# A batched matrix product in fp32: weights of four matrices in one load, quarter-lane casts on two engines, and no block around the engine programs

## The chip, the cores and the metric

The kernel runs on one core of a Trainium2 chip. A core has engines that run their own instruction streams and meet through semaphores: TensorE (matrix products, PE in the profile, with its weight loads as PEld), VectorE (DVE), ScalarE (ACT), GpSimd (POOL) and SyncE (SP), and 16 DMA engines that move data between HBM and the on-chip memory SBUF. Matrix products land in a second on-chip memory, PSUM. The metric is the device time of one execution in microseconds, as the median over runs.

## The reference

```python
def setup_inputs():
    b1, b2, m, k, n = 8, 16, 256, 512, 384
    return {
        "x": np.random.randn(b1, b2, m, k).astype(np.float32),
        "weight": np.random.randn(b1, b2, k, n).astype(np.float32),
    }

def reference(x: np.ndarray, weight: np.ndarray) -> np.ndarray:
    return np.matmul(x, weight).astype(np.float32)
```

There are 128 independent products, each of 256 x 512 by 512 x 384. In bytes: 67 MB of x, 101 MB of weights, 50 MB of output.

## The kernel before

**Tiling.** The 128 matrices are taken in 32 groups (`NG`) of four (`G`). Of one group, x is 1024 rows of 512; each of the 128 partitions holds 8 consecutive rows (`R`), so that 32 partitions (`C`) hold one matrix. A group is worked in four quarters (`T`), each of two rows per partition. The loads are `x_sb` (2 MB, two buffers), and `w_sb` (1.5 MB, four buffers): one load of weights has two matrices (`D`), and in it a partition holds 8 consecutive weight rows, a run of 12 KB. A group has two such loads. The output of a group is one store of 1.5 MB, from four buffers `out_sb`.

**Stages.** For a group n, in the order of the data:

- `cast_x` on ScalarE (lines 125 to 136) turns x from fp32 to bf16 and reorders its columns on the way, in two instructions of 2048 elements per partition. There is one buffer `x_bf`; the wait of line 128 is for the transposes of group n-1.
- `prepare` on VectorE (lines 138 to 157) first casts the weights into `w_bf` (two groups' worth of buffers): eight instructions, each on 64 partitions with 1536 elements. The two halves of a matrix go to the upper and the lower partitions, which makes the order of the contraction index agree with that of x. It waits for the product of group n-2 (line 140) and for each load (line 143).
- `multiply` on TensorE (lines 159 to 187) transposes the four quarters of x, two bf16 values at a time as one fp32 word, into PSUM buffers `pt` (four).
- The second half of `prepare` (lines 152 to 156) copies these transposes to `x_t` in SBUF, a quarter at a time. It stands behind the weight casts on VectorE.
- `multiply` then makes the product: per quarter 32 matmuls, each with a 128 x 32 block of `x_t` as stationary and 128 x 384 of weights as moving operand. The four matrices of a group sit in four column blocks of the array. Results are in two PSUM buffers `po`, so that quarter q+2 waits for the copy-out of quarter q (line 176).
- `copy_out` on ScalarE (lines 190 to 198) moves a quarter to `out_sb`. Behind the second quarter of group n, ScalarE does `cast_x` of group n+1.

**The order of transfers** is written by hand on SyncE, the only issuer (lines 209 to 224). `load` (lines 96 to 113) issues x of a group, then its two halves of the weights; x waits for the cast of x two groups back (line 99), each half of the weights for the casts of that half two groups back (line 107). SyncE issues the loads of groups 0 to 3 (`LAG`), and then for each n the load of group n+4 and the store of group n. The last store goes out in four pieces. All transfers stand in one queue, in the order of issue.

**Frame.** The engine programs are functions inside an `nc.Block()` (line 200), which stands in a critical section of the tile framework (line 54). In the profile, instructions of the section's entry and exit have line 54, those of the block's exit the helper file's line, and those of the program's end line 288.

Of the kernel before, what the change touches and what calls it, by code (L numbers as in the profile page):

```python
# [11 lines left out]
def kernel(  # L12
# [25 lines left out]

# [4 lines left out]
    D = 2  # L43
    S = 2
    HP = P // D
    NG = B // G

    XS, WS, OS = 2, 2 * G // D, 4
    BS, TS, WBS = 1, 2, 2 * G
# [4 lines left out]
    ctx.enter_context(tc.tile_critical())  # L54
# [11 lines left out]
    def sems(name, n):  # L66
# [5 lines left out]

    x_bf = sbuf("x_bf", [P, R, S, HP, KO], bf16, BS)
    x_t = sbuf("x_t", [P, R, KO // 2, P, 2], bf16, TS)
    w_sb = sbuf("w_sb", [P, S * KO, N], fp32, WS)
    w_bf = sbuf("w_bf", [P, KO, N], bf16, WBS)
# [7 lines left out]
    id_done, x_cast, w_cast, t_made, t_copied, p_made, o_copied = (  # L84
        sems(name, 1)[0]
        for name in (
            "id_done", "x_cast", "w_cast", "t_made", "t_copied", "p_made", "o_copied"
# [8 lines left out]
    def load(e, t, U, s):  # L96
        n = t * U + s
        if not isinstance(n, int) or n >= XS:
            e.wait_ge(x_cast, n + (1 - XS))
# [4 lines left out]
        for d in range(G // D):  # L104
            slot = (s * (G // D) + d) % WS
            if not isinstance(n, int) or n >= 2:
                e.wait_ge(w_cast, n * (G * S) + ((d + 1) * D * S - 2 * G * S))  # L107
            e.dma_start(  # L108
                w_sb[slot][:],
                w_rows[bass.ds(n * (G * K) + d * (D * K), D * K)].rearrange(  # L110
                    "(p k) n -> p k n", k=S * KO
                ),
            ).then_inc(w_in[slot], 16)
# [11 lines left out]
    def cast_x(e, t, U, s):  # L125
        n = t * U + s
        e.wait_ge(x_in[s % XS], (t * (U // XS) + s // XS) * 16 + 16)
        e.wait_ge(t_made, n * T + ((1 - BS) * T + BIAS))
        for h in range(S):
            ins = e.copy(  # L130
                out=x_bf[s % BS][:, :, h],
                in_=x_sb[s % XS][:].rearrange("p r (q s c) -> p r s q c", s=S, c=KO)[
                    :, :, h
                ],
            )
        ins.then_inc(x_cast, 1)

    def prepare(e, t, U, s):
        n = t * U + s
        e.wait_ge(p_made, n * T + (BIAS - T))  # L140
        for d in range(G // D):
            slot = (s * (G // D) + d) % WS
            e.wait_ge(  # L143
# [46 lines left out]
    def copy_out(e, t, U, s, q):  # L190
        n = t * U + s
        if q == 0:
# [4 lines left out]
            in_=po[(s * T + q) % PO][:, :, :N],  # L197
        ).then_inc(o_copied, 1)

    block = ctx.enter_context(nc.Block())  # L200

    @block.gpsimd
    def _(e):
# [89 lines left out]
```

## Time and profile before

| | us |
|---|---|
| median of 14 runs (lowest to highest) | 519.99 (519.63 to 520.25) |
| the profiled execution | 520.48 |
| its span, first to last instruction | 518.7 |
| TensorE busy (matmul) | 313.1 |
| VectorE busy | 323.9 |
| ScalarE busy | 212.7 |
| GpSimd busy | 0.7 |

The profile is of one execution. Its span leaves out what lies before the first and after the last instruction, here 1.8 us. A row of the instruction groups reads: line, engine, operation, output<-input, shapes, count | busy us, mean ns of one | idle time of the engine just before, and what ended most of it. The slices cut the span into 40 equal parts of 13 us; each digit is a busy share in tenths.

The transfers by issue, with KB each and the median us from issue to landing, are:

```profile
w_sb<-in_weight_dram SPq DMA_DIRECT2D x64, 1536.0 KB, 27.5
x_sb<-in_x_dram SPq DMA_DIRECT2D x32, 2048.0 KB, 25.9
out_dram<-out_sb SPq DMA_DIRECT2D x31, 1536.0 KB, 30.6
out_dram<-out_sb SPq DMA_DIRECT2D x4, 384.0 KB, 3.9
```

A landing time of some 27 us for transfers that take 4 to 5 us of the engines' time says that a transfer waits in the queue behind others.

### The profile page before, as it was taken

Reading aid. Unit: us, or ns where it says so; the run is one execution under the profiler, and the core shown is the slowest. Engines: PE = TensorE matmul, PEld = TensorE weight load, DVE = VectorE, ACT = ScalarE, POOL = GpSimd, SP = SyncE. Lnnn points to the kernel's source line nnn. Section 1 sums busy time; section 2 is a strip of 40 time slices with the busy share of each in tenths; the row PEclk is TensorE's granted clock in tenths of the full one; section 3 lists DMA queues with packets and bytes.
Section 4 is the critical chain, followed back from the end, with each engine's and each line's share of the span. In section 5 each row is a group of like instructions: output and inputs, shape, how many; then the busy total and the mean of one; then the engine's idle time right before and its main releaser. Section 6 shows DMA issues by size and latency. Waiting matters only on the chain.

```text
span 518.7 us, 11239 instructions
## 1 busy us (share of the span) xinstructions
PE 313.1 (60%) x4608; PEld 197.2 (38%) x4608; DVE 323.9 (62%) x384; ACT 212.7 (41%) x193; POOL 0.7 (0%) x6
## 2 busy tenths in 40 slices
PE   0685864576655666555766557665576655676653
PEld 0453542343433443334434334343344333443431
DVE  0878867655577555775556765557755577555670
ACT  3073662454324553245533345523455224553332
POOL 0000000000000000000000000000000000000000
PEclk9798897787868886787768678866888678777867
DMA  8999999999999999999999999999999999999995
GB/s 332 431 427 425 426 429 427 429 430 428 428 430 425 432 427 429 431 428 432 428 426 427 431 431 430 424 429 430 430 429 427 429 429 426 432 426 428 430 428 207
DMA packets 18868, 218.16 MB, mean 421 GB/s; under 512 B 2096, under 2 KB 2096, under 8 KB 2608
## 3 DMA queue, kind: packets, MB, share of 16 engines
q1 hardware_dynamic: 18864, 218.11, 99.1%
q8 instruction: 2, 0.03, 0.0%
q14 instruction: 2, 0.02, 0.0%
HBM read 167.77 MB, written 50.33 MB: 420 GB/s over the span
## 4 chain that ended last, share of the span: by engine, by line
DMA 80%; DVE 12%; issue 3%; PE 2%; ACT 1%; SPq 0%; DVEq 0%; ACTq 0%
DMA w_sb<-in_weight_dram 80%; DVE w_bf L148 12%; PE po L181 2%; ACT x_bf L130 0%; DVEq _compat.py:109 0%; SPq L108 0%; ACT out_sb L195 0%; SPq L100 0%; DVE x_t L154 0%; DVEq L143 0%; DVEq L230 0%; SPq L107 0%; ACTq L194 0%; SPq L288 0%; SPq L54 0%
## 5 line engine op out<-in xcount | busy, mean ns | idle before, releaser
L148 DVE CAST w_bf<-w_sb 64x1536 bf16<-64x1536 f32 x256 | 244.5, 955 | 179.8 <-DMA w_sb<-in_weight_dram 167.2
L181 PE MATMUL po<-w_bf,x_t 128*32 128x384 bf16 x4096 | 233.2, 402 | 124.7 <-DVE x_t L154 124.7
L195 ACT COPY out_sb<-po 128x768 f32<-128x768 f32 x128 | 99.2, 802 | 291.1 <-PE po L181 291.1
L181 PEld LDWEIGHTS po<-w_bf,x_t 128*32 128x32 bf16 x4096 | 125.9, 117 | 228.4 <-DVE x_t L154 133.5
L167 PE MATMUL pt<-identity,x_bf 128*128 128x128 f32 x512 | 80.0, 317 | 72.7 <-ACT x_bf L130 72.7
L130 ACT CAST x_bf<-x_sb 128x2048 bf16<-128x2048 f32 x64 | 118.4, 1901 | 6.2 <-DMA x_sb<-in_x_dram 6.2
L167 PEld LDWEIGHTS pt<-identity,x_bf 128*128 128x128 f32 x512 | 71.3, 212 | 84.6 <-issue 84.6
L154 DVE COPY x_t<-pt 128x1024 bf16<-128x1024 bf16 x128 | 79.4, 683 | 1.0
L130 ACT ACT_TABLE_LOAD x1 | 1.3, 1283 | 1.3 <-PEq L237 1.3
masks.py:199 POOL TENSOR_SCALAR_AFFINE_SELECT identity<-identity 128x128 f32<-128x128 f32 x1 | 0.3, 292 | 0.2 <-POOL identity L204 0.2
L204 POOL MEMSET identity<- 128x128 f32 x1 | 0.2, 205 | 0.5 <-SPq L54 0.5
L277 POOL MEMSET const-bfloat16-1.0<- 128x1 bf16 x1 | 0.1, 101 | 0.0
L277 POOL MEMSET const-uint8-127<- 128x1 uint8 x1 | 0.1, 101 | 0.0
L277 POOL MEMSET const-float32-0.0<- 128x1 f32 x1 | 0.1, 98 | 0.2 <-issue 0.2
L277 POOL MEMSET const-float32-1.0<- 128x1 f32 x1 | 0.1, 98 | 0.0
## 6 DMA issues: line engine op xcount, KB each, us to landing
w_sb<-in_weight_dram SPq DMA_DIRECT2D x64, 1536.0 KB, 27.5
x_sb<-in_x_dram SPq DMA_DIRECT2D x32, 2048.0 KB, 25.9
out_dram<-out_sb SPq DMA_DIRECT2D x31, 1536.0 KB, 30.6
out_dram<-out_sb SPq DMA_DIRECT2D x4, 384.0 KB, 3.9
```

Source lines behind the costliest of these rows:

```text
L130: ins = e.copy(out=x_bf[s % BS][:, :, h], in_=x_sb[s % XS][:].rearrange("p r (q s c) -> p r s q c", s=S, c=KO)[:, :, h],)
L148: e.tensor_copy(out=w_bf[(s * G + d * D + a) % WBS][h * HP : (h + 1) * HP], in_=w_sb[slot][a * HP : (a + 1) * HP, h * KO : (h + 1) * KO, : ...
L154: e.tensor_copy(out=x_t[s % TS][:, 2 * q : 2 * q + 2], in_=pt[(s * T + q) % PT][:].bitcast(bf16),).then_inc(t_copied, 1)
L167: ins = e.transpose(pt[(s * T + q) % PT][:, rr, h, :], words[:, 2 * q + rr, h :: KO // 2], identity[:],)
L181: ins = e.matmul(po[(s * T + q) % PO][mine, rr, :N], x_t[s % TS][:, 2 * q + rr, ko // 2, mine, ko % 2], w_bf[(s * G + i) % WBS][:, ko, :], ...
L195: e.copy(out=out_sb[s % OS][:, 2 * q : 2 * q + 2, :], in_=po[(s * T + q) % PO][:, :, :N],).then_inc(o_copied, 1)
L204: e.memset(identity[:], 0.0).then_inc(id_done, 1)
L277: nc = _bacc.Bacc("TRN2", target_bir_lowering=False, num_devices=1)
```

## The change

The engine programs become plain functions that are called one after another on their engines inside the critical section; the block is gone, and the section is told not to drain GpSimd at its end. The weights of a group come as one load of 3 MB, in which 32 partitions hold one matrix and each partition a run of 16 rows, 24 KB; `w_sb` has two such buffers, as many bytes as before. Since a partition now holds 16 consecutive rows of the contraction index, a matrix is cast in four pieces of 32 partitions (quarters h), and x is reordered in fours instead of twos (`s=G`). VectorE casts three quarters of each matrix (12 instructions a group), ScalarE the fourth (4 instructions a group), with a semaphore for each (`v_cast`, `a_cast`). On ScalarE, the casts of matrices 0 and 1 of group n+1 stand ahead of the copy-outs of group n, those of matrices 2 and 3 behind them. The cast of x is cut into quarters, one behind each copy-out, and `x_cast` counts quarters. `x_t` has one buffer instead of two. For the last group the weights are loaded ahead of x, for which one round of SyncE's loop is written out.

```diff
-    D = 2
-    S = 2
-    HP = P // D
+    V = G - 1
-    XS, WS, OS = 2, 2 * G // D, 4
-    BS, TS, WBS = 1, 2, 2 * G
+    XS, WS, OS = 2, 2, 4
...
-    ctx.enter_context(tc.tile_critical())
+    ctx.enter_context(tc.tile_critical(no_gpsimd_drain=True))
...
-    x_bf = sbuf("x_bf", [P, R, S, HP, KO], bf16, BS)
-    x_t = sbuf("x_t", [P, R, KO // 2, P, 2], bf16, TS)
-    w_sb = sbuf("w_sb", [P, S * KO, N], fp32, WS)
+    x_bf = sbuf("x_bf", [P, R, G, C, KO], bf16, 1)[0]
+    x_t = sbuf("x_t", [P, R, KO // 2, P, 2], bf16, 1)[0]
+    w_sb = sbuf("w_sb", [P, G * KO, N], fp32, WS)
...
+    def load_w(e, t, U, s):
+        n = t * U + s
+        if not isinstance(n, int) or n >= WS:
+            e.wait_ge(v_cast, (n - WS + 1) * (G * V))
+            e.wait_ge(a_cast, (n - WS + 1) * G)
+        e.dma_start(
+            w_sb[s % WS][:],
+            w_rows[bass.ds(n * (G * K), G * K)].rearrange("(p k) n -> p k n", k=G * KO),
+        ).then_inc(w_in[s % WS], 16)
+
+    def load(e, t, U, s):
+        order = (load_w, load_x) if isinstance(t, int) and s == NG - 1 else (load_x, load_w)
+        for part in order:
+            part(e, t, U, s)
...
+    def cast_x(e, t, U, s, q):
+        n = t * U + s
+        if q == 0:
+            e.wait_ge(x_in[s % XS], (t * (U // XS) + s // XS) * 16 + 16)
+        e.wait_ge(t_made, n * T + (q + 1 - T + BIAS))
+        rows = slice(2 * q, 2 * q + 2)
+        e.copy(
+            out=x_bf[:, rows],
+            in_=x_sb[s % XS][:, rows].rearrange(
+                "p r (q s c) -> p r s q c", s=G, c=KO
+            ),
+        ).then_inc(x_cast, 1)
+
+    def cast_w(e, cast, t, U, s, i, parts, done):
+        for h in parts:
+            cast(
+                out=w_bf[(s * G + i) % (2 * G)][h * C : (h + 1) * C],
+                in_=w_sb[s % WS][i * C : (i + 1) * C, h * KO : (h + 1) * KO, :],
+            ).then_inc(done, 1)
+
+    def cast_w_start(e, t, U, s):
+        n = t * U + s
         e.wait_ge(p_made, n * T + (BIAS - T))
+        e.wait_ge(w_in[s % WS], (t * (U // WS) + s // WS) * 16 + 16)
...
     def multiply(e, t, U, s):
-        e.wait_ge(x_cast, n + 1)
         for q in range(T):
+            e.wait_ge(x_cast, n * T + (q + 1))
             e.wait_ge(t_copied, n * T + (q + 1 - PT + BIAS))
...
-        e.wait_ge(w_cast, n * (G * S) + G * S)
+        e.wait_ge(v_cast, n * (G * V) + G * V)
+        e.wait_ge(a_cast, n * G + G)
...
-    block = ctx.enter_context(nc.Block())
-
-    @block.sync
-    def _(e):
+    def on_sync(e):
...
-        rounds = (NG - LAG) // U
+        rounds = (NG - LAG) // U - 1
...
+    def on_vector(e):
...
+                cast_w_start(e, t, U, s)
+                for i in range(G):
+                    cast_w(e, e.tensor_copy, t, U, s, i, range(V), v_cast)
+                evacuate(e, t, U, s)
...
+    def on_scalar(e):
...
+        def casts(t, U, s, group):
+            if group[0] == 0:
+                cast_w_start(e, t, U, s)
+            for i in group:
+                cast_w(e, e.copy, t, U, s, i, range(V, G), a_cast)
+
         def step(t, U, s, more):
+            if more:
+                casts(t, U, s + 1, (0, 1))
             for q in range(T):
                 copy_out(e, t, U, s, q)
-                if q == 1 and more:
-                    cast_x(e, t, U, s + 1)
+                if more:
+                    cast_x(e, t, U, s + 1, q)
+            if more:
+                casts(t, U, s + 1, (2, 3))
...
+        for q in range(T):
+            cast_x(e, 0, NG, 0, q)
+        casts(0, NG, 0, (0, 1, 2, 3))
...
+    on_gpsimd(nc.gpsimd)
+    on_sync(nc.sync)
+    on_vector(nc.vector)
+    on_tensor(nc.tensor)
+    on_scalar(nc.scalar)
```

## The prediction

> **What bounds the kernel now.** I read the page's slices first, then the DMA queues, the groups of instructions, and last, for the ends, the table of windows, the timeline and SyncE's waits.
>
> ```profile
> span 518.7 us, 11239 instructions
> ...
> DMA  8999999999999999999999999999999999999995
> GB/s 332 431 427 425 426 429 427 429 430 428 428 430 425 432 427 429 431 428 432 428 426 427 431 431 430 424 429 430 430 429 427 429 429 426 432 426 428 430 428 207
> DMA packets 18868, 218.16 MB, mean 421 GB/s; under 512 B 2096, under 2 KB 2096, under 8 KB 2608
> ...
> q1 hardware_dynamic: 18864, 218.11, 99.1%
> ```
>
> The reader is to see that from slice 2 to slice 39 the 16 DMA engines never rest. 218.11 MB at 428 GB/s is 510 us of the 518.7. Whatever the change does inside the stream is hidden unless it alters the bytes, the time per byte, or lets the queue run dry. Only the first and last slice are open.
>
> ```profile
> L148 DVE CAST w_bf<-w_sb 64x1536 bf16<-64x1536 f32 x256 | 244.5, 955 | 179.8 <-DMA w_sb<-in_weight_dram 167.2
> L195 ACT COPY out_sb<-po 128x768 f32<-128x768 f32 x128 | 99.2, 802 | 291.1 <-PE po L181 291.1
> L130 ACT CAST x_bf<-x_sb 128x2048 bf16<-128x2048 f32 x64 | 118.4, 1901 | 6.2 <-DMA x_sb<-in_x_dram 6.2
> L154 DVE COPY x_t<-pt 128x1024 bf16<-128x1024 bf16 x128 | 79.4, 683 | 1.0
> ```
>
> VectorE waits 167.2 us for weights: compute is paced by the loads. Weights land every 15.97 us per group in the landings of the trace, and that is the budget of a group.
>
> The end, in 1 us windows (PE, PEld, DVE, ACT, POOL, then clock, DMA share, GB/s):
>
> ```profile
> 506.00:507.00 1.00, 1.00 (x20) 0.50 (x16) 0.00 (x0) 0.65 (x1) 0.00 (x0) 0.50 1.01 430
> 509.00:510.00 1.00, 1.00 (x34) 0.61 (x25) 0.00 (x0) 0.75 (x1) 0.00 (x0) 1.00 0.62 246
> 515.00:516.00 1.00, 0.00 (x0) 0.00 (x0) 0.00 (x0) 0.00 (x0) 0.00 (x0) 0.50 0.06 25
> ```
>
> SyncE's own waits there (us in total, times, longest):
>
> ```profile
> SPq L224 <- DMA out_dram<-out_sb: 5.3, 2, 3.7
> ```
>
> A share of 0.06 is one engine of sixteen. The landings say the same: the last weights are in on the median engine at 493.9 us and on the slowest at 497.93; its last store lands at 517.05, 19.1 us later. After 507 us most engines wait for results while this one still works off a backlog of stores. So the kernel ends with the slowest DMA engine, not with compute: the last copy-out ends at 511.35.
>
> **What the Trainium skill says.** "DMA: Bandwidth & Descriptors", "Why small descriptors are slow (HBM only)", has a small fixed overhead for every packet. The trace agrees: followed engine by engine, load packets start 607.1 ns apart at 16 KB and 456.5 ns at 12 KB, so 36.8 ns per 1000 bytes and about 5 ns fixed; a semaphore packet takes 6 ns. "ScalarE: Activation LUTs", "What ACT_TABLE_LOAD costs", prices an activation with immediates at 186 ns + 0.833 ns per element, with 93 ns overlap back to back. The trace agrees: 2048 elements are 1901 ns (formula 1892), and two take 3.70 us. "VectorE: DVE Perf Modes", the section on the TRN2 errata, prices an SBUF operation by a fixed term and elements per partition, with no term for the number of partitions.
>
> **The change part by part.** Zero is the landing of the group's weights; eight casts take 7.86 us in the timeline, so 0.983 us each; four PSUM copies 2.48.
>
> *Block and drain.* In the trace SyncE's branch into the block costs about 0.1 us ahead of the first load (issued at 0.97), and between the end of its last wait (517.10) and the critical section's end (517.53) lies a branch and an all-engine barrier of 0.4. Both go: -0.5 us. GpSimd's drain there is 0.03 us. Bounds 0 and -0.8.
>
> *24 KB runs.* Per group and DMA engine, 16 packets of 12 KB become 8 of 24 KB, and 3 semaphore packets stand where 4 did: 8 x 4.8 + 6 = 44 ns, times 32 groups = -1.4 us. No 24 KB packet is in this trace. Bounds: 0, if the slowest engine (12 KB in 459 ns median, up to 494) is held by something else; -2.1, if the 7.5 ns intercept of the packet durations (460 and 611) is taken.
>
> *Quarter casts.* VectorE: 12 x 0.983 + 2.48 = 14.3 us a group instead of 10.3. A 32-lane cast isn't in the trace; I take 955 ns as for 64 lanes, since the 256 casts at all lane offsets lie in 951 to 960. Upper bound: at 1.12 us each it reaches 15.97. ScalarE: a cast of 1536 elements is 186 + 0.833 x 1536 = 1466, 1.37 back to back; x quarters (1024) 1.04, 0.94 back to back. Per group 4 x 1.37 + 4 x 0.94 + 4 x 0.75 = 12.2 us. TensorE stays at 313.1 / 32 = 9.8. All are under 15.97, and what hides them is the stream.
>
> *The new waits.* ScalarE now waits for the weights of group n+1 ahead of copy-out n; queued behind it are four copies, the x casts and two more weight casts, for which TensorE and SyncE wait. Steady state: two casts to 2.75, copies and x casts interleaved to 9.8, last casts to 12.5; VectorE to 11.8, evictions to 14.3. So x of n+2 is issued at about 10 and its weights at 12.5 after landing n. At landing n the queue still holds store n-4, x and w of n+1, store n-3: 3.7 + 4.9 + 7.3 + 3.7 = 19.6 us. Cover 7 us; if it were gone, each late us would idle all engines. Store n, queued on SyncE behind both loads, has its results long before.
>
> *Start.* The first weights come as one 3 MB load, complete at 16.1 instead of 12.4. Casts to 27.9, product 0 from 28.65, its quarters ready at 31.5, 33.9, 35.2, 36.6; ScalarE has cast half of w(1) by 31.2, and finishes x(1) at 39.1. So x(3) is issued at 39.2 instead of 30.77, first data 1.05 us later (as 0.97 to 2.0 at the start): 40.3. The median engine runs dry about 39.7, the slowest 1.6 later: bubble 0.6 on most, 0 on the one that counts; the next group again 0.4. I take +0.2, bounds 0 and +1.5.
>
> *End.* The last group loads w ahead of x. Zero is now x(31)'s landing on the slowest engine; w(31) lands at -4.9, w(30) at -15.95. VectorE: casts(30) to -4.15, evictions to -1.65, casts(31) to +10.1; the product follows the start of the evictions by 0.75 (502.25 to 503.00): 10.85. ScalarE is done with its casts at 9.2, so VectorE sets the start. The last product takes 7.5 us (503.0 to 510.55 before; idle gap ahead similar), end 18.35; copy to 19.2; the last store lands 2.3 after its issue on an engine with no backlog (511.37 to 513.63): 21.5. The backlog that covers this ends at 19.1 as before, so compute shows: +2.4 us. If the product runs at its 5.4 us of 33.4 to 38.8, it is +0.3. Bounds +0 and +3.
>
> Sum: 518.7 - 0.5 - 1.4 + 0.2 + 2.4 = 519.4 of span; with the 1.78 us around the span (520.48 - 518.7) 521.2, against 520.48 profiled: +0.7. The median of the runs, 519.99, is 0.5 under the profiled execution; the difference applied to it gives 520.7 us.
>
> **Rivals.** (1) *Faster*: the last product runs at full clock, or the store backlog hides it, and the packet saving is whole. Then -0.5 - 1.4 + 0.2 + 0.3 = -1.4: 518.6, and 517.9 with the 2.1. For it: matmuls do reach 326 ns in the trace; against: clock 0.50 in the windows ahead of the last product. (2) *Slower, one mechanism*: the queue runs dry at the start. x(3) stands behind x_cast(1), behind half of w(1)'s casts and product 0. It decides once x(3)'s first data comes after the slowest engine is dry, 41.3; a ScalarE or product 0 later by 2 to 3 us than summed gives 1 to 2 us of idle, on top of +0.7: 521.7 to 522.7. Against: 1 us of margin, from durations of this trace. (3) *Compute becomes the bound*: 32-lane casts at over 1.12 us. Each 0.1 above costs 1.2 us a group, some 35 us in all; against it the row of 955. Chance 0.03. (4) *The change doesn't do what it says*: 24 KB runs are cut into smaller packets; then the 1.4 is given back: 522.1. It counts in the slower case.
>
> **How the numbers follow.** About 0.2%, 1.0 us, is what can be told from no change here. Central case, within 0.2% (518.9 to 521.0): 0.45. Faster by rival 1: 0.23. Slower by rivals 2, 4, the upper bound of the end, and 3: 0.32. The single bounds rarely fall together; the range from rival 1 at 518.2 to rival 2 at 522.4 leaves out about 2 in 10. The central case's own range is 519.4 to 521.0.
>
> **What would show it.** Packets about 14,260 (18,864 - 4,096 - 512), with 24 KB ones near 913 ns; DMA tenths still 9 in the inner slices; VectorE at 12 x 32 casts of about 955 ns, busy 446 us; ScalarE about 410. In the last slice, the last product starting some 11 us after x(31)'s landing and the final store landing about 2.3 us after issue with no single engine lagging behind it. Wrong if an inner slice of the DMA row falls under 9, if x(3) leaves a hole near 40 us, if the last product still ends ahead of the backlog, or if 24 KB packets take other than 908 to 915 ns.

## The result, and the profile after

| | before | after |
|---|---|---|
| median of the runs (lowest to highest), us | 519.95 (519.63 to 520.25) | 526.84 (526.71 to 527.74) |
| the profiled execution, us | 520.48 | 526.82 |
| its span, us | 518.7 | 524.6 |

After takes 1.0137 times as long as before, with a 95% interval of 1.0127 to 1.0147: 6.9 us slower. The forecast was 520.7 with a range up to 522.4. It was wrong, and wrong in the direction of rival 2, the queue that runs dry at the start.

The page of after, with its slices, queues and groups:

```profile
span 524.6 us, 11696 instructions
...
PE 334.2 (64%) x4608; PEld 211.5 (40%) x4608; DVE 444.6 (85%) x512; ACT 409.0 (78%) x385; POOL 0.7 (0%) x6
...
DMA  8999999999999999999999999999999999999993
GB/s 344 432 423 401 369 402 425 434 427 433 439 430 424 429 429 432 434 428 430 430 429 436 432 430 426 429 431 441 428 430 424 430 434 433 429 430 375 384 429 159
DMA packets 14260, 218.16 MB, mean 416 GB/s; under 512 B 1584, under 2 KB 1584, under 8 KB 2096
...
q1 hardware_dynamic: 14256, 218.11, 98.1%
...
L144 DVE CAST w_bf<-w_sb 32x1536 bf16<-32x1536 f32 x384 | 365.2, 951 | 68.3 <-DMA w_sb<-in_weight_dram 51.9
...
L144 ACT CAST w_bf<-w_sb 32x1536 bf16<-32x1536 f32 x128 | 187.9, 1468 | 84.8 <-DMA w_sb<-in_weight_dram 79.6
...
L135 ACT CAST x_bf<-x_sb 128x1024 bf16<-128x1024 f32 x128 | 134.2, 1050 | 7.3 <-DMA x_sb<-in_x_dram 6.5
```

Every size that the prediction gave for the work itself is there: 14,260 packets, casts of 951, 1468 and 1050 ns, VectorE 444.6 us busy. The row of tenths shows nothing: it is all nines. The row under it does: slices 4 to 6 (39 to 79 us) carry 401, 369 and 402 GB/s where before carried 425 to 429. A 9 stands for 90% or more, so that an idle us or so in a slice of 13 leaves no mark; the bytes moved do. The late dip (375 and 384) will turn out to cost nothing.

The hole itself, in windows of after (start and end, us, then PE, PEld, DVE, ACT, POOL, clock, DMA share, GB/s):

```profile
39.00:40.00 1.00, 0.28 (x3) 0.09 (x1) 0.97 (x2) 0.98 (x2) 0.00 (x0) 1.00 1.08 246
...
52.00:53.00 1.00, 0.27 (x2) 0.27 (x3) 0.97 (x2) 0.97 (x2) 0.00 (x0) 1.00 0.25 107
53.00:54.00 1.00, 0.47 (x4) 0.28 (x3) 0.97 (x2) 1.00 (x1) 0.00 (x0) 1.00 0.76 156
54.00:56.00 2.00, 0.00 (x0) 0.00 (x0) 1.94 (x3) 1.95 (x3) 0.00 (x0) 1.00 0.68 238
64.00:66.00 2.00, 2.00 (x44) 1.25 (x37) 1.94 (x3) 2.00 (x4) 0.00 (x0) 1.00 1.13 381
66.00:68.00 2.00, 1.36 (x11) 1.17 (x11) 1.94 (x3) 1.98 (x4) 0.00 (x0) 1.00 0.84 301
```

The share and the GB/s count a packet whole where it starts, so a share can pass 1. At 52 to 53 us few packets start any more: the queue runs empty, and at 53.5 us one of the 16 engines is still at work. While this goes on, VectorE is busy 0.97 of every us and ScalarE as much: the queue waits for compute. Note the first line: a share of 1.08 with 246 GB/s. There the engines are busy but slow. SyncE's timeline shows what was issued into the hole (start, us, engine, line, transfer):

```profile
38.44 0.33 SPq L98 DMA_DIRECT2D x_sb<-in_x_dram  x1
42.24 0.33 SPq L108 DMA_DIRECT2D w_sb<-in_weight_dram  x1
52.80 0.35 SPq L98 DMA_DIRECT2D x_sb<-in_x_dram  x1
56.70 0.34 SPq L108 DMA_DIRECT2D w_sb<-in_weight_dram  x1
57.34 0.36 SPq L125 DMA_DIRECT2D out_dram<-out_sb  x1
```

These are x(3), w(3), x(4), w(4) and store 0. In the kernel before, x(3) and x(4) went out at 30.77 and 40.89. w(3) has landed on the median engine at 52.95, and x(4), issued at 52.80, has its first data at 53.80. SyncE's waits say for whom it stood (us in total, times, longest):

```profile
SPq L98 <- ACT x_bf L135: 326.8, 29, 12.6
SPq L107 <- ACT w_bf L144: 91.6, 30, 14.8
...
SPq L225 <- DMA out_dram<-out_sb: 1.9, 1, 1.9
```

The first is the wait of a load of x for ScalarE's cast of x two groups back. That total of 326.8 us is no loss as such: in the steady state it is covered by the transfers still queued. The last line is the end, where the wait for the last stores is down from 5.3 us to 1.9: no engine with a backlog is left to wait for.

**Where the 5.9 us of span come from.** A transfer has 16 landings, one for each DMA engine. Below, "median engine" is the median of the 16 and "slowest engine" the last of them, read in both traces. Three differences add up:

| place | before | after | difference, us |
|---|---|---|---|
| x(8) lands, median engine | 121.01 | 124.11 | +3.1 |
| x(8) lands, slowest engine | 122.77 | 126.38 | +3.6 |
| per group from x(8) to x(30), median engine | 15.891 | 15.811 | -0.08 |
| per group from x(8) to x(30), slowest engine | 15.992 | 15.986 | 0 |
| w(30) lands, slowest engine | 481.94 | 485.35 | **+3.4** |
| from there to the last store's landing | 35.11 | 37.85 | **+2.75** |
| from there to the end of the span | 1.66 | 1.44 | **-0.2** |

3.4 + 2.75 - 0.2 is the 5.9 between the spans. So the start costs 3.4 to 3.6, the end 2.75, the frame gives 0.2 back, and no gain of the packets is seen on the engine that counts.

### The profile page after: what moved, and what is told of

It reads as the page before. It is cut to its first block, busy times and chain, and to the rows that moved or that the text cites. A ratio compares the mean times of both kernels' runs of the same rounds, so it can differ in the third digit from the quotient of the medians.

```text
span 524.6 us, 11696 instructions
## 1 busy us (share of the span) xinstructions
PE 334.2 (64%) x4608; PEld 211.5 (40%) x4608; DVE 444.6 (85%) x512; ACT 409.0 (78%) x385; POOL 0.7 (0%) x6
## 2 busy tenths in 40 slices
DMA packets 14260, 218.16 MB, mean 416 GB/s; under 512 B 1584, under 2 KB 1584, under 8 KB 2096
## 4 chain that ended last, share of the span: by engine, by line
DMA 48%; ACT 15%; issue 14%; DVE 12%; PE 9%; ACTq 0%; SPq 0%; DVEq 0%
DMA w_sb<-in_weight_dram 48%; DVE w_bf L144 10%; PE po L186 8%; ACT w_bf L144 8%; ACT out_sb L200 4%; ACT x_bf L135 3%; DVE x_t L158 2%; PE pt L171 1%; ACTq L199 0%; SPq L108 0%; ACTq L133 0%; SPq L98 0%; ACTq L271 0%; DVEq L230 0%; SPq L107 0%
## 5 line engine op out<-in xcount | busy, mean ns | idle before, releaser
L144 DVE CAST w_bf<-w_sb 32x1536 bf16<-32x1536 f32 x384 | 365.2, 951 | 68.3 <-DMA w_sb<-in_weight_dram 51.9
L186 PE MATMUL po<-w_bf,x_t 128*32 128x384 bf16 x4096 | 254.0, 419 | 157.4 <-DVE x_t L158 63.9
L144 ACT CAST w_bf<-w_sb 32x1536 bf16<-32x1536 f32 x128 | 187.9, 1468 | 84.8 <-DMA w_sb<-in_weight_dram 79.6
L186 PEld LDWEIGHTS po<-w_bf,x_t 128*32 128x32 bf16 x4096 | 143.2, 120 | 260.4 <-DVE x_t L158 101.7
L135 ACT CAST x_bf<-x_sb 128x1024 bf16<-128x1024 f32 x128 | 134.2, 1050 | 7.3 <-DMA x_sb<-in_x_dram 6.5
L200 ACT COPY out_sb<-po 128x768 f32<-128x768 f32 x128 | 102.3, 799 | 18.4 <-PE po L186 17.7
L171 PE MATMUL pt<-identity,x_bf 128*128 128x128 f32 x512 | 82.3, 303 | 28.4 <-ACT x_bf L135 28.3
L171 PEld LDWEIGHTS pt<-identity,x_bf 128*128 128x128 f32 x512 | 68.3, 208 | 47.7 <-issue 46.4
## 6 DMA issues: line engine op xcount, KB each, us to landing
x_sb<-in_x_dram SPq DMA_DIRECT2D x32, 2048.0 KB, 14.3
```

The lines of the kernel that those rows point to most:

```text
L135: e.copy(out=x_bf[:, rows], in_=x_sb[s % XS][:, rows].rearrange("p r (q s c) -> p r s q c", s=G, c=KO),).then_inc(x_cast, 1)
L144: cast(out=w_bf[(s * G + i) % (2 * G)][h * C : (h + 1) * C], in_=w_sb[s % WS][i * C : (i + 1) * C, h * KO : (h + 1) * KO, :],).then_inc(do ...
L171: ins = e.transpose(pt[(s * T + q) % PT][:, rr, h, :], words[:, 2 * q + rr, h :: KO // 2], identity[:],)
L186: ins = e.matmul(po[(s * T + q) % PO][mine, rr, :N], x_t[:, 2 * q + rr, ko // 2, mine, ko % 2], w_bf[(s * G + i) % (2 * G)][:, ko, :], sta ...
L200: e.copy(out=out_sb[s % OS][:, 2 * q : 2 * q + 2, :], in_=po[(s * T + q) % PO][:, :, :N],).then_inc(o_copied, 1)
```

## The experiments

"Idle" and "slowed" in this section are worked out from the packets between 30 and 110 us: idle is the time in which DMA engines had no packet, slowed the time that packets took above the usual duration of their size (about 611 ns at 16 KB, 462 at 12 KB, 914 at 24 KB; counted where over 6% more), both divided by 16. All runs are set against the kernel before on the same chip, at 519.84 to 520.01.

### The frame and the packets, each alone

The kernel before without the block and without GpSimd's drain:

```diff
-    ctx.enter_context(tc.tile_critical())
+    ctx.enter_context(tc.tile_critical(no_gpsimd_drain=True))
...
-    block = ctx.enter_context(nc.Block())
...
-    @block.sync
-    def _(e):
+    def on_sync(e):
...
+    on_sync(nc.sync)
```

> The kernel before with the engine programs straight in the critical section and no GpSimd drain; all else as before. Theory: the block's exit barrier is all it saves, 0.26 us of the end of the trace (1.65 us from the last landing to the end before, 1.39 after): 519.7. First estimate of the prediction: -0.5, 519.45. Rival: nothing, the exit is hidden in what lies around the span: 519.95.

Measured: 519.65 us (519.44 to 520.03), ratio 0.9995 [0.9987, 1.0004]. From the last store's landing to the end of the span it is 1.44 us instead of 1.66, exactly as in after; the first load is still issued at 0.96 to 0.97. The gain is some 0.2 us, at the end only, and the ratio's interval holds 1: as a time it isn't shown, as a piece of the trace it is.

After, with each load of weights cut into two loads of 12 KB runs that are waited for together:

```diff
-        e.dma_start(
-            w_sb[s % WS][:],
-            w_rows[bass.ds(n * (G * K), G * K)].rearrange("(p k) n -> p k n", k=G * KO),
-        ).then_inc(w_in[s % WS], 16)
+        rows = w_rows[bass.ds(n * (G * K), G * K)].rearrange("(p k) n -> p k n", k=G * KO)
+        for j in range(2):
+            part = slice(j * 2 * KO, (j + 1) * 2 * KO)
+            e.dma_start(w_sb[s % WS][:, part], rows[:, part]).then_inc(
+                w_in[s % WS + WS * j], 16
+            )
```

> The changed kernel with each 3 MB load of weights as two loads of 12 KB runs (the two halves of each partition's rows), both waited for where the one was. Theory: the slowest DMA engine keeps its pace of 15.98 us a group whatever the packets, so they are worth nothing to the end: 526.6 to 527.1, with the median engine 0.08 us a group slower. Rival, the prediction's step: packets cost 44 ns a group on every engine: +1.4, 528.2.

Measured: 527.66 us (527.04 to 528.58), between the two expectations. Per group it needs 15.887 us on the median engine, the value of before, where after has 15.811: the larger runs do save 0.08 us a group there, more than the 0.044 predicted. The slowest engine needs 16.05. Over the kernels of this study that the transfers bind, that engine has been at 15.96 to 16.08 with runs of either size, which over 22 groups is a scatter of over 2 us, more than the saving. So the packets' saving is shown on the median engine and not in the time: on the slowest engine it is neither seen nor excluded.

### The end

After, with x ahead of the weights for the last group too:

```diff
-        order = (load_w, load_x) if isinstance(t, int) and s == NG - 1 else (load_x, load_w)
-        for part in order:
+        for part in (load_x, load_w):
```

> The changed kernel with x ahead of the weights for the last group too. Theory: the end hangs on VectorE's chain from the landing of group 30's weights, and the hole in the DMA row at 482 to 486 us lies beside it; with x first that hole closes, but the last weights land some 1.7 us after VectorE is free: +1.5 to +2, 528.3 to 528.9. Rival: the hole, made by x waiting on SyncE behind the wait of the weights, is part of the loss: -1.3 to -2, about 525.

Measured: 529.27 us (527.39 to 530.03), +2.4 against after and 0.4 above the range expected. VectorE's timeline of this kernel; then the last product from TensorE's timeline, and 1 us in the midst of it as a window (the granted clock is the third number from the end):

```profile
485.61 11.75 DVE L143 CAST w_bf<-w_sb 32x1536 bf16<-32x1536 f32 x12 [1.64 <-DMA w_sb<-in_weight_dram]
497.39 2.48 DVE L157 COPY x_t<-pt 128x1024 bf16<-128x1024 bf16 x4
501.72 11.75 DVE L143 CAST w_bf<-w_sb 32x1536 bf16<-32x1536 f32 x12 [1.84 <-DMA w_sb<-in_weight_dram]
```

```profile
515.22 5.38 PE L185 MATMUL po<-w_bf,x_t 128*32 128x384 bf16 x128 [2.46 <-ACT w_bf L143]
```

```profile
517.00:518.00 1.00, 1.00 (x35) 0.72 (x26) 0.00 (x0) 0.60 (x1) 0.00 (x0) 1.00 0.00 0
```

And of after, in the same order:

```profile
485.37 11.76 DVE L144 CAST w_bf<-w_sb 32x1536 bf16<-32x1536 f32 x12 [1.64 <-DMA w_sb<-in_weight_dram]
497.16 2.48 DVE L158 COPY x_t<-pt 128x1024 bf16<-128x1024 bf16 x4
499.67 11.76 DVE L144 CAST w_bf<-w_sb 32x1536 bf16<-32x1536 f32 x12
511.46 2.48 DVE L158 COPY x_t<-pt 128x1024 bf16<-128x1024 bf16 x4
```

```profile
512.21 7.80 PE L186 MATMUL po<-w_bf,x_t 128*32 128x384 bf16 x128 [2.70 <-DVE x_t L158]
```

```profile
514.00:515.00 1.00, 1.00 (x16) 0.48 (x12) 0.00 (x0) 0.00 (x0) 0.00 (x0) 0.50 0.06 25
```

This chain sets the end of after: from w(30)'s landing on the slowest engine VectorE never rests until the last product, and the last casts start when VectorE is free, not when w(31) comes. ScalarE is close behind: its last casts for that product end at 511.62, 0.6 before it starts. With x first w(31) is late enough (501.63) that both wait for it: ScalarE's last casts end at 514.88, and the last product starts at 515.22, 3.0 later than in after. That execution is only 0.6 us longer than after's, and the shortest of its four, because its last product takes 5.38 us and not 7.80: the clock granted to TensorE is 1.00 all through it, and 0.50 in after's from 512 to 517 us. In the medians the order for the last group is worth 2.4 us, given these casts. The late hole in the stream of after (482 to 486 us, x(31) behind the wait of w(31) on SyncE) isn't what costs: with x first slices 37 and 38 carry 431 and 426 GB/s, and the time is longer.

After, with the weights in two halves of 12 KB runs with semaphores of their own; VectorE casts quarters 0 and 1 of all matrices, then quarter 2:

```diff
+            if not isinstance(n, int) or n >= WS:
+                e.wait_ge(v_cast, (n - WS) * (G * V) + (2 * G if j == 0 else G * V))
+                if j == 1:
+                    e.wait_ge(a_cast, (n - WS + 1) * G)
...
+                for j, parts in enumerate((range(2), range(2, V))):
+                    w_landed(e, t, U, s, j)
+                    for i in range(G):
+                        cast_w(e, e.tensor_copy, t, U, s, i, parts, v_cast)
```

> The changed kernel with each load of weights in two halves of 12 KB runs, each with its own semaphore; VectorE casts two quarters of each matrix from the first half as soon as it is there, the third from the second, and each half of a buffer is loaded again when its own casts are done. ScalarE still waits for the second half ahead of the copy-outs. Theory, formed after the last runs: two chains of the same length hold back x of group 3, VectorE's casts of the first weights (to 28.7 us) and ScalarE's wait for the weights of group 1 (to 28.3 and on to 31.2); to shorten VectorE's alone leaves x(3)'s issue at 38.4 and gives about 1 us at x(4). VectorE's last chain starts 3.6 us earlier, which takes most of the 2.75 us of the end: 523.0 to 524.8. Rival, that VectorE's chain alone makes the start: the whole 3.6 and the end, about 520.5.

Measured: 526.79 us (526.05 to 530.93), the same as after. x(3) and x(4) went out where the expectation had them (38.60 and 51.89), the idle time fell from 1.79 to 0.71 us, the slowed time stayed at 2.34, and x(8) landed only 0.5 us earlier. At the start the miss was to price a hole by its idle time alone. At the end the chain hardly got shorter: VectorE's last evictions begin 0.9 us earlier than in after (510.52), but ScalarE's last casts now end at 512.97, and the last product starts at 513.31, 26.4 us after w(30)'s landing on the slowest engine where after had 26.9.

### The start: one chain at a time

In after, x(n+2) waits for x(n)'s cast on ScalarE, that for the copy-outs of group n-1, and those for the product, which waits for VectorE's casts and evictions. The next runs shorten one piece at a time. First, VectorE casts only half the columns of each piece in groups 0 to 3:

```diff
+        for n in range(4):
+            cast_w_start(e, 0, NG, n)
+            for i in range(G):
+                cast_w(e, e.tensor_copy, 0, NG, n, i, range(V), v_cast, 2)
+            evacuate(e, 0, NG, n)
```

> The changed kernel with VectorE casting only half of the columns of its weight pieces in groups 0 to 3 (the other half of those products' weights is zero or stale, so their output isn't the reference's); VectorE's share of a group there falls from 14.3 to 9.5 us. Theory: the start is lost because compute frees a buffer only every 14.3 us while the loads of a group without a store take 12.2; with less work the holes at 39 and 53 us shrink, though ScalarE's chain of casts, copies and x casts still stands: -1.3 to -2.5, 524.3 to 525.5. Rival: the loss is the later landing of the first weights as one load, which this leaves: no change, 526.8.

Measured: 526.63 us (526.03 to 527.45), no gain that can be told from after. x(3) is even issued at 39.07. Product 0 is early, but ScalarE's timeline has the copy-outs where they were:

```profile
28.22 2.96 ACT L144 CAST w_bf<-w_sb 32x1536 bf16<-32x1536 f32 x2 [6.17 <-DMA w_sb<-in_weight_dram]
31.21 0.80 ACT L200 COPY out_sb<-po 128x768 f32<-128x768 f32 x1
```

ScalarE waits 6.17 us for w(1), the new wait ahead of copy-out 0. There are two nearly equal chains, and taking one away shows next to nothing. So the other way: all four of ScalarE's casts go behind the copy-outs, in every group.

```diff
         def step(t, U, s, more):
-            if more:
-                casts(t, U, s + 1, (0, 1))
...
-                casts(t, U, s + 1, (2, 3))
+                casts(t, U, s + 1, (0, 1, 2, 3))
```

> The changed kernel with all four of ScalarE's weight casts of group n+1 behind the copy-outs of group n, so that no copy-out waits for weights. Theory of two equal chains: nothing is gained at the start, as product 0 begins at 28.7 on VectorE's account: 526.3 to 527.5. Rival, that ScalarE's new wait alone makes the start: -3, about 523.8.

Measured: 551.13 us (550.33 to 551.38), +24. This I hadn't expected. ScalarE's and TensorE's timelines of a group in mid-stream:

```profile
202.60 5.94 ACT L144 CAST w_bf<-w_sb 32x1536 bf16<-32x1536 f32 x4
211.69 0.80 ACT L200 COPY out_sb<-po 128x768 f32<-128x768 f32 x1 [3.14 <-PE po L186]
...
219.31 5.95 ACT L144 CAST w_bf<-w_sb 32x1536 bf16<-32x1536 f32 x4
228.40 0.80 ACT L200 COPY out_sb<-po 128x768 f32<-128x768 f32 x1 [3.14 <-PE po L186]
```

```profile
208.89 8.00 PE L186 MATMUL po<-w_bf,x_t 128*32 128x384 bf16 x128 [5.44 <-DVE w_bf L144]
```

The copy-outs come every 16.71 us, more than the 15.97 of a group's transfers, though no engine is busy as long. The product starts at 208.89, 0.35 after ScalarE's four casts end at 208.54; the trace names VectorE's casts for this wait, but those of this group had ended at 201.9. It is a ring: the product waits for ScalarE's casts, the copy-outs for the product, and the next casts stand behind the copy-outs. In after, two of the four stand ahead of them and lie under the product. The next two runs, one with the lighter casts of VectorE and one with the halves and x first for the last group, have the same ring:

```diff
-                casts(t, U, s + 1, (2, 3))
+                casts(t, U, s + 1, (0, 1, 2, 3))
...
+                cast_w(e, e.tensor_copy, 0, NG, n, i, range(V), v_cast, 2)
```

> The last two ideas together on the changed kernel: ScalarE's weight casts behind the copy-outs, and VectorE casting half of the columns of its pieces in groups 0 to 3 (the rest of those weights is zero or stale, so the output of those groups isn't the reference's). Theory of two equal chains: x(3) is issued at 33 to 34 and x(4) at about 48, no hole in the DMA row at 39 and 53 us, and no slowed packets behind the holes; the start's 3.6 us go, the end's stay: 523.0 to 524.2. Rival, that the start is lost to something that neither touches (the packets of 24 KB, the single load): 526 to 527.

Measured: 546.32 us (545.22 to 547.17). The time only shows the ring; the start is readable all the same: with both chains shortened x(3) is issued at 34.06, over 4 us earlier than in after, and the hole near 39 us is gone. The rest of the expectation failed here too: x(4) goes out at 50.94, not at about 48, and a hole stays at 53 us.

```diff
-                casts(t, U, s + 1, (2, 3))
+                casts(t, U, s + 1, (0, 1, 2, 3))
...
-        order = (load_w, load_x) if isinstance(t, int) and s == NG - 1 else (load_x, load_w)
-        for part in order:
+        for part in (load_x, load_w):
...
+                    w_landed(e, t, U, s, j)
```

> The changed kernel with the weights in two halves with their own semaphores as in the first run of this set, ScalarE's weight casts behind the copy-outs, and x ahead of the weights for the last group too. Both chains of the start are shorter (VectorE's by 3.6 us) and after the last landing VectorE has four casts left. Theory: no hole at the start, the end hidden behind the slowest engine's stores, no block: 519.3 to 520.2, about the kernel before. Rival: the start or the end has another cause and 1 us or more stays: over 521.

Measured: 547.13 us (546.58 to 547.34), the ring again. It says nothing on halves or on the order.

To have the start without the ring, the next three make changes in the first groups only. The casts behind the copy-outs in the first two rounds of ScalarE:

```diff
+        for n in range(U):
+            step(0, NG, n, True, behind=n < 2)
+        with e.Fori(0, NG // U - 2) as t:
+            for s in range(U, 2 * U):
```

> The changed kernel with ScalarE's weight casts behind the copy-outs in the first two steps alone; the rest of its order stays. Theory of two chains: product 0 still begins at 28.7 on VectorE's account, x(3) is issued at 38.4 as before, and the casts of groups 1 and 2 end later, so weights 3 and 4 are issued 2 us later: 526.8 to 528.5, no gain. Rival, that ScalarE's wait alone makes the start: 523.5 to 524.5.

Measured: 531.00 us (530.33 to 531.39), 4.2 more than after and above the 526.8 to 528.5 expected. x(3) is issued at 38.49, as VectorE's chain has it; the ring, in these two rounds, pushes w(3) from 42.24 to 44.52 and x(4) from 52.80 to 55.30. The page of this kernel:

```profile
GB/s 341 436 422 382 278 376 423 411 440 429 429 427 431 429 438 432 427 426 432 427 439 430 428 430 429 430 434 432 434 423 432 428 436 435 429 423 392 384 412 205
```

Slice 5 (53 to 66 us) is down to 278. x(8) lands 4.1 us later than in after on the slowest engine, and the profiled execution is 3.5 us longer: most of what is lost at the start is passed on.

The weights of groups 0 and 1 in two loads, so that VectorE's casts start with the first half:

```diff
+        if isinstance(n, int) and n < WS:
+            half = 2 * KO
+            e.dma_start(w_sb[s][:, :half], rows[:, :half]).then_inc(w_first[s], 16)
+            e.dma_start(w_sb[s][:, half:], rows[:, half:]).then_inc(w_in[s], 16)
```

> The changed kernel with the weights of groups 0 and 1 alone in two loads of 12 KB runs with their own semaphores, so that VectorE starts its casts at 12.4 instead of 16.1 us; all later loads as they were. Theory of two chains: ScalarE still waits for all of the weights of group 1 ahead of its first copy-out, x(3) is issued at 38.3, x(4) at 51.5 instead of 52.8: -0.8 to -1.5, 525.3 to 526.1. Rival, that VectorE's late start alone makes it: 523.2 to 524.

Measured: 526.05 us (525.19 to 526.26), as expected: VectorE's part of the chain alone is worth little.

Both of these together:

```diff
+            e.dma_start(w_sb[s][:, :half], rows[:, :half]).then_inc(w_first[s], 16)
...
+            step(0, NG, n, True, behind=n < 2)
```

> Both edits of the two kernels beside it together. Theory: x(3) is issued at about 34, x(4) at 49.5, the weights of group 4 at 55.5; no hole at 39, at most 1 us at 53 to 56; the start's loss falls from 3.6 to about 1, the end's 2.8 us stay: 523.8 to 524.8. Rival, that the start is lost to something that neither touches: 526.3 or more.

Measured: 525.94 us (525.74 to 526.47), not the 523.8 to 524.8 expected. x(3) is early (35.31) and the hole at 39 gone, but the ring takes it back one group on: x(4) at 51.45, w(4) at 57.46 (after: 56.70).

Both engines cast half the columns, VectorE in groups 0 to 5, ScalarE in groups 0 to 4:

```diff
+        for n in range(6):
...
+                cast_w(e, e.tensor_copy, 0, NG, n, i, range(V), v_cast, 2)
...
-                cast_w(e, e.copy, t, U, s, i, range(V, G), a_cast)
+                ko = 2 if isinstance(t, int) and s < 5 else KO
+                cast_w(e, e.copy, t, U, s, i, range(V, G), a_cast, ko)
```

> The changed kernel with both engines casting half of the columns of their weight pieces at the start: VectorE in groups 0 to 5, ScalarE in groups 0 to 4 (the rest of those weights is zero or stale, so the output of those groups isn't the reference's); the order of everything stays. VectorE then takes 9.5 us a group, and the loop from a product over the last copy-out and x cast and two weight casts to the next product about 11.1 instead of 13.0, both under the 12.2 us of a group's loads. Theory: the queue doesn't run dry before the first store, no hole and no slowed packets at 39 and 53 us, x of group 8 lands at about 120.5 us on the median engine instead of 124.1, and the kernel is 3.0 to 3.6 faster: 523.2 to 523.9; what stays is the end. Rival, that the start is lost to the loads themselves (24 KB runs, 3 MB at once): x of group 8 still at 124, 526.3 or more.

Measured: 524.39 us (523.01 to 525.79), a part of the start's loss back. The expectation for x(8) failed: 123.22 on the median engine and not 120.5, since x(4) still comes late (50.59; w(2) lands at 40, and ScalarE's casts and copy-outs stand between).

### The start: the wait of x taken away

What was open then: is it the dry queue that costs, or are the first groups slower because of the 24 KB runs? The run with two loads of 12 KB each speaks against the second already: without any packet of 24 KB its x(8) lands at 124.21 and 126.42 us (median and slowest engine), as late as in after. A third buffer of x moves the disputed wait one group back. SyncE's and ScalarE's loops are written out for it, since three buffers don't divide into a loop of four; the first run is that alone, as a control.

```diff
-        with e.Fori(0, rounds) as t:
-            for s in range(U):
-                load(e, t, U, LAG + s)
-                store(e, t, U, s)
-        for n in range(rounds * U, NG):
+        for n in range(NG):
...
-        for n in range(NG - U, NG):
+        for n in range(NG):
             step(0, NG, n, n < NG - 1)
```

> The changed kernel with the loops of SyncE and ScalarE written out, nothing else: the control for the next two. Both theories expect no change: 526.5 to 527.2.

Measured: 526.15 us (525.51 to 526.82). This is what the next two stand against.

```diff
-    XS, WS, OS = 2, 2, 4
+    XS, WS, OS = 3, 2, 4
```

> The same with three buffers of x instead of two, so that the load of x(n+3), and no longer that of x(n+2), waits for the cast of x(n). Theory (what is lost at the start is lost because the queue runs dry): x(3) and x(4) go out right behind w(2) and w(3), the holes at 39 and 52 us are gone, and one is left where w(4), issued at 56.7 as before, has its first data at 57.7 while the queue is dry from about 55.8. About half of the 3.1 us that x(8) lands late is given back: 525.0 to 525.8, x(8) at 122 to 123 on the median engine. Rival (the first groups are slow because of the 24 KB runs or of the weights' layout, whatever stands in the queue): x(8) at 124 and 526.8.

Measured: 526.64 us (525.39 to 527.95), no gain, and not the 525.0 to 525.8 expected. The two holes are gone, the one forecast at 56 to 58 us is there: 0.87 us idle, and 2.38 slowed, as much as in after. x(8) is 1.6 us earlier than the control's on the median engine (123.33 against 124.96), but the slowest engine is where it was (125.95 against 126.06).

With the first two groups' weights in halves besides:

```diff
-    XS, WS, OS = 2, 2, 4
+    XS, WS, OS = 3, 2, 4
...
+            e.dma_start(w_sb[s][:, :half], rows[:, :half]).then_inc(w_first[s], 16)
+            e.dma_start(w_sb[s][:, half:], rows[:, half:]).then_inc(w_in[s], 16)
```

> The same, and the weights of groups 0 and 1 in two halves, so that VectorE starts earlier and w(4) goes out at about 54.8 instead of 56.7. Theory: no hole is left, the DMA tenths are 9 from slice 2 on, x(8) lands at 121.0 to 121.5 on the median and about 123 on the slowest engine, as in the kernel before, and the time falls by the whole 3.1 to 3.6 us of the start: 523.2 to 523.9. Rival as above: x(8) no earlier than 123.2, time 526 or more.

Measured: 523.88 us (522.10 to 524.20), ratio to before 1.0065 [1.0043, 1.0087], against the control's 1.0117. SyncE's timeline and, in a second fence, windows of this kernel:

```profile
24.48 0.43 SPq L99 DMA_DIRECT2D x_sb<-in_x_dram  x1
41.68 0.33 SPq L115 DMA_DIRECT2D w_sb<-in_weight_dram  x1
42.05 0.43 SPq L99 DMA_DIRECT2D x_sb<-in_x_dram  x1
54.57 0.33 SPq L115 DMA_DIRECT2D w_sb<-in_weight_dram  x1
```

```profile
52.00:54.00 2.00, 0.38 (x4) 0.19 (x2) 1.94 (x3) 1.98 (x2) 0.00 (x0) 0.97 1.02 434
54.00:56.00 2.00, 1.16 (x16) 0.71 (x20) 1.97 (x5) 1.97 (x2) 0.00 (x0) 0.50 1.04 442
62.00:64.00 2.00, 2.00 (x36) 1.49 (x29) 1.94 (x3) 2.00 (x3) 0.00 (x0) 1.00 1.14 295
```

x(3) and x(4) go out at 24.48 and 42.05, w(4) at 54.57 as forecast, and where after had its hole the engines move 434 GB/s. Idle is 0.15 us. x(8) lands at 121.56 and 123.37, against 121.01 and 122.77 before: nearly the whole start is back, with the 24 KB runs in place from group 2 on. (The halves of groups 0 and 1 are 12 KB runs, but on their own they left x(8) at 126.23.) The 0.6 left are in the third window: at 62 to 64 us packets are slow with no hole ahead of them. What slows them isn't known: after has them at 64 to 68 us, shortly before its first store's data, the run with 12 KB loads has as much of it (0.84 us between 61 and 70), and neither the kernel before nor the one without a block has any to speak of (0.02).

All of it in one table. The last column is the profiled execution's time less x(8)'s landing on the slowest engine:

| kernel | x(3), x(4) issued | idle | slowed | x(8): median, slowest | profiled time | the rest |
|---|---|---|---|---|---|---|
| before | 30.77, 40.89 | 0.06 | 0.16 | 121.01, 122.77 | 520.48 | 397.7 |
| after | 38.44, 52.80 | 1.79 | 2.34 | 124.11, 126.38 | 526.82 | 400.4 |
| light on VectorE | 39.07, 52.06 | 1.41 | 2.78 | 124.19, 126.60 | 527.45 | 400.9 |
| behind, first two rounds | 38.49, 55.30 | 3.81 | 5.07 | 128.95, 130.45 | 530.33 | 399.9 |
| first weights in halves | 38.51, 51.80 | 0.60 | 2.68 | 123.46, 126.23 | 526.26 | 400.0 |
| these two together | 35.31, 51.45 | 1.05 | 2.93 | 124.16, 126.38 | 525.85 | 399.5 |
| light on both engines | 37.04, 50.59 | 0.60 | 2.19 | 123.22, 124.32 | 524.79 | 400.5 |
| loops written out | 39.01, 53.31 | 2.12 | 2.65 | 124.96, 126.06 | 526.56 | 400.5 |
| three x buffers | 28.17, 42.47 | 0.87 | 2.38 | 123.33, 125.95 | 526.28 | 400.3 |
| three, and halves | 24.48, 42.05 | 0.15 | 1.30 | 121.56, 123.37 | 524.10 | 400.7 |

The rest is 399.5 to 400.9 us in all these variants, whatever their start, and 397.7 before: the start is told well by one number, the landing of x(8) on the slowest engine, and what comes later adds 1.8 to 3.2 us, about the 2.75 of the end. No run takes the end away alone; its cause is read from the timelines above.

## Why the prediction was wrong

**Block and drain** (-0.5): the step was a term too large. -0.2, all of it at the exit. The branch ahead of the first load, counted at 0.1, stays: the first load is issued at 0.96 to 0.97 with or without a block.

**24 KB runs** (-1.4): it failed as a time, at its own lower bound, "0, if the slowest engine is held by something else". On the median engine the saving is 0.08 us a group; on the slowest, which the prediction itself had named as the one that ends the kernel, 15.99 and 15.99 in the two executions. The prediction gave the saving of an ordinary engine to the slowest one, whose own pace scatters by more than that from run to run.

**Quarter casts**: right in each number. They are hidden in the steady state, VectorE's 14.3 us behind the transfers' 15.97.

**The new waits**, and with them **the start** (+0.2, bounds 0 and +1.5): here the prediction failed: 3.4 us at w(30)'s landing where 0.2 stood. The issue times in it were good: x(3) at 39.2 and measured 38.44, VectorE's first casts to 27.9 and measured 27.91, product 0 at 28.65 and measured 28.69. Four things around them were not:

- The budget of 15.97 us holds 3.7 for a store. The first store is issued behind the loads of group 4, at 57.34; until then a group is 12.2 us of transfers (4.9 and 7.3), and VectorE's period of 14.3 is above that, not below. The "19.6 us of queue" that covers the new wait counts two stores that don't exist yet. So the start isn't one slip of 0.6 and one of 0.4: it is a deficit of 2 us for each group until the stores come, and x(4) finds a larger hole than x(3). Asking when the queue runs dry with the transfers that are issued by then, group by group, would have told.
- The bubbles, "0.6 on most" and "the next group again 0.4", were the wrong way round and had no slow packets in them. On the median engine the data of w(2) ends at 39.5 us, near the 39.7 forecast, and x(3)'s first packet starts at 39.43: idle is only 0.26 us there (37 to 46 us), but 0.70 goes to slowed packets. At x(4) it is 1.47 idle and 0.73 slowed (50 to 61 us). Such times have to be read from the packets, since a landing comes later: w(2) lands at 39.95, some 0.45 after its last data. "DMA: Bandwidth & Descriptors", "Anatomy of one DMA — SWDGE (gpsimd) path", in the Trainium skill says that the semaphore of a transfer waits for the receipt of the last byte; these loads are issued by SyncE and show such a delay, though not its reason.
- "0 on the one that counts": the slowest engine's lag was taken for a cover. More than half of the lag is indeed used up at the second hole (1.5 us at w(3), 0.65 at x(4)), but at x(8) it is 2.3 again, and x(8) lands 3.6 us later there, more than on the median. Why it comes back isn't shown.
- A hole was priced by its idle time. After is idle for 1.79 us between 30 and 110 us, and spends 2.34 on slowed packets: the 0.70 and 0.73 at the two holes, and 0.76 at 61 to 70 us with no hole ahead. Less the 0.22 that before has of both, and the 0.6 that the larger runs save in eight groups, this makes 3.3 us by estimate, near the 3.1 by which the median engine lands x(8) later. The run in halves (idle down by 1.1, time unchanged) and the third buffer (idle halved, time unchanged) show that the idle part alone tells little.

**The end** (+2.4): right in mechanism and nearly in size, 2.75. From w(30)'s landing on the slowest engine to the last store the prediction's steps give 15.95 + 21.5 = 37.45 us, measured 37.85; 0.3 of the rest is the last product's 7.80 where 7.5 stood. In the kernel before this stretch took 35.1, set by the stores of the slowest engine. The granted clock under the last product is in this term: at a clock of 1.00, as rival 1 had it, the product takes 5.38 us in the run with x first.

**Rivals**: rival 2 gave the mechanism and its place, with "1 us of margin" against it. Its point of decision, that x(3)'s first data comes after the slowest engine is dry, wasn't reached: 39.43 against 41.08, and at x(4) 53.80 against 54.01. The loss came all the same, so the last engine to run dry was the wrong one to ask. Its price, 1 to 2 us, came from looking at x(3) alone. With 3.4 for 0.2 in the sum, 0 for the -1.4 of the packets, -0.2 for the -0.5 of the frame and 2.75 for the 2.4 of the end, the span is 519.4 + 3.2 + 1.4 + 0.3 + 0.35 = 524.65, and 524.6 was measured. The forecast of the median then lacks another 0.9: around the span lie 2.2 us and not 1.78, and the 0.5 by which before's median was under its profiled execution isn't there in after. Rival 3 (compute becomes the bound) didn't come, with casts of 951 ns, nor did rival 4, with 14,260 packets.

**Left open**: why packets are slow at a restart and again at 62 to 68 us; how much of the end would go if both VectorE's and ScalarE's last casts were shorter; and whether the packets' saving would reach the time on a core whose slowest engine isn't slower than the rest. None of the variants is faster than the kernel before beyond what can be told apart: the one without a block is at 0.9995, with 1 in its interval.

## What to carry to other kernels

A kernel that is bound by its transfers in the steady state has a start in which the queue holds fewer kinds of them: set the period of each compute engine against what is in the queue then, not against the steady budget, and follow it group by group until the first store. Where two engines form a ring with a buffer between them, shortening one side alone showed next to nothing here, and moving work "behind" can close a ring that is longer than any engine's busy time. When a transfer-bound kernel is compared by its landings, use the engine that lands last: the saving on the median engine didn't show in the time here.

## What the runs showed of the hardware

- **A queue that ran dry restarts slowly.** Most of the first packets after a hole take 1.0 to 1.7 us where 16 KB take 0.61 otherwise. In after this costs 0.70 and 0.73 us per engine at its two holes, about what it costs at the program's start (0.84 between 2 and 6 us).
- **From issue to first data** it is 0.96 to 1.05 us for SyncE's loads into an empty queue, of which 0.33 to 0.39 is the issuing instruction. "DMA: Bandwidth & Descriptors", "Latency and other measured facts", has about 600 ns for the first byte on that path. This agrees if it is counted from the end of the issuing instruction (0.63 to 0.69 us here); for the size of a hole the whole 1.0 us from the issue counts.
- **One DMA engine is slower than the others**, with 15.96 to 16.08 us a group against 15.81 to 15.89 on the median, in the kernel before as in the others that the transfers bind, whatever the size of the runs. At x(30) the last of the 16 landings is 4.0 us behind the median in before and 6.1 in after, the last but one 1.7 and 2.4.
- **VectorE's cast** of 1536 elements takes 951 ns on 32 partitions and 955 on 64: the number of partitions has no price in these two.
- **The same product of 128 matmuls** takes 5.38 us (the end of the run with x first, in its profiled execution) to 8.26 us (group 2 of after). The granted clock is 1.00 throughout the first, and 0.50 in the second from 57 to 62 us. At the end of a kernel that is on the path; that it makes a part of the scatter between the executions is likely, but not shown.
